# A tiled 8192 x 8192 transpose: TensorE's program half in two-turn loops, with a semaphore for each PSUM bank

## The chip, the cores and the metric

One core of a Trainium2 chip runs the kernel. The metric is the device time of one execution in microseconds (us), median of several runs. Ratios are the mean time of one kernel's fast runs over the mean of the other's fast runs of the same rounds, so they are not quite the ratio of the medians quoted here. Profiles are of one execution; their span is about 1.8 us shorter than the time.

## The reference

```python
def setup_inputs():
    return {"x": np.random.randn(8192, 8192).astype(np.float32)}

def reference(x):
    return np.transpose(x)
```

268.4 MB are read and 268.4 MB are written. There is no arithmetic.

## The kernel before

The input is cut into 128 chunks of 128 rows x 4096 columns (2 MiB). A chunk is loaded to one of three input buffers. TensorE transposes its 32 squares of 128 x 128, four to a PSUM bank, eight banks in all. ScalarE copies the even banks and VectorE the odd ones to store regions in SBUF; a region gathers the same output rows over eight chunks, so that a store writes long rows. One region is full after each chunk and is stored (2 MiB). Nine regions serve eight open windows. SyncE issues all loads and stores, on one queue.

```python
for t, (s, c) in enumerate(chunks):
    nc.tensor.wait_ge(s_ld[t % NIN], 16 * (t // NIN + 1))
    closing = []
    for q in [(c + k) % NR for k in range(NR)]:       # the closing bank first
        if q not in window:
            ...                                        # take a free region r
            if stored[r]:
                (nc.scalar, nc.vector)[q % 2].wait_ge(s_st[r], 16 * stored[r])
        ...
        if bank[n % NPS] is not None:
            nc.tensor.wait_ge(*bank[n % NPS])          # count of the copying engine
        for b in range(B):
            last = nc.tensor.transpose(...)
        last.then_inc(s_pe, 1)
        n += 1
        (nc.scalar, nc.vector)[e].wait_ge(s_pe, n)
        ...                                            # copy the bank to its region
        cp.then_inc(s_cp[e], 1)
        ...
    for q, e, count in closing:
        nc.sync.wait_ge(s_cp[e], count)
        ...                                            # store the region
    if t + NIN < len(chunks):
        nc.sync.wait_ge(s_pe, n)
        load(t + NIN)
```

Of the kernel before, what the change touches and what calls it, by code (L numbers as in the profile page):

```python
# [24 lines left out]
def wide_dma(nc, eng, queue, out, in_):  # L25


    return eng.add_instruction(
        mybir.InstDMACopy(
            mode="Copy",  # L30
            name=nc.get_next_instruction_name(),
            engine=eng.engine,
            ins=[physical(in_)],
            outs=[physical(out)],
            queue=queue,
        )
    )


@with_exitstack  # L40
def kernel(
    ctx: ExitStack,
    tc: tile.TileContext,
    x: bass.AP,
    out: bass.AP,
):






    nc = tc.nc
    P = 128
    N, M = x.shape
    assert x.shape == out.shape[::-1]
    dt = x.dtype

    S = 32
    B = 4  # L60
    W = 8
    NR = S // B
    NIN = 3
    NREG = 9
    NPS = 8
    CH = N // P
    J = S * P

    with tc.tile_critical():  # L69
        nc.alloc_sbuf_tensor("pad", [P, 32], dt)  # L70
        ident = nc.alloc_sbuf_tensor("ident", [P, P], dt).ap()
        ins = [nc.alloc_sbuf_tensor(f"in{k}", [P, J], dt).ap() for k in range(NIN)]
        regs = [nc.alloc_sbuf_tensor(f"reg{k}", [P, B * W * P], dt).ap() for k in range(NREG)]
        pss = [nc.alloc_psum_tensor(f"ps{k}", [P, B * P], dt).ap() for k in range(NPS)]

        s_id = nc.alloc_semaphore("s_id")
        s_ld = [nc.alloc_semaphore(f"s_ld{k}") for k in range(NIN)]
        s_st = [nc.alloc_semaphore(f"s_st{k}") for k in range(NREG)]
        s_pe = nc.alloc_semaphore("s_pe")
        s_cp = [nc.alloc_semaphore("s_cpa"), nc.alloc_semaphore("s_cpv")]  # L80

        nc.gpsimd.memset(ident, 0.0).then_inc(s_id, 1)  # L82
        nc.gpsimd.wait_ge(s_id, 1)
        nc.gpsimd.affine_select(  # L84
            out=ident,
            in_=ident,
            compare_op=mybir.AluOpType.not_equal,
            fill=1.0,
            base=0,
            pattern=[[-1, P]],  # L90
            channel_multiplier=1,
        ).then_inc(s_id, 1)
        nc.tensor.wait_ge(s_id, 2)

        chunks = [(s, c) for s in range(M // J) for c in range(CH)]

        def load(t):
            s, c = chunks[t]
            nc.sync.dma_start(
                out=ins[t % NIN], in_=x[c * P:(c + 1) * P, s * J:(s + 1) * J]  # L100
            ).then_inc(s_ld[t % NIN], 16)

        for t in range(NIN):
            load(t)

        n = 0
        copied = [0, 0]
        bank = [None] * NPS
        free = list(range(NREG))
        stored = [0] * NREG  # L110
        window = {}
        stores = 0
        for t, (s, c) in enumerate(chunks):
            nc.tensor.wait_ge(s_ld[t % NIN], 16 * (t // NIN + 1))
            closing = []
            for q in [(c + k) % NR for k in range(NR)]:
                if q not in window:


                    span = (q - c) % W + 1  # L120
                    r = free.pop(0)
                    parts = [(s, c, min(c + span, CH))]
                    if c + span > CH and t + span < len(chunks):
                        parts.append((s + 1, 0, c + span - CH))
                    window[q] = (t, r, parts)
                    if stored[r]:
                        (nc.scalar, nc.vector)[q % 2].wait_ge(s_st[r], 16 * stored[r])
                t0, r, parts = window[q]
                k = [p[0] for p in parts].index(s)
                base = B * P * sum(z - a for _, a, z in parts[:k])  # L130
                _, a, z = parts[k]
                rows = (z - a) * P
                view = regs[r][:, base:base + B * rows].rearrange("p (b i) -> p b i", b=B)
                ps = pss[n % NPS]
                e = q % 2
                if bank[n % NPS] is not None:
                    nc.tensor.wait_ge(*bank[n % NPS])
                for b in range(B):
                    last = nc.tensor.transpose(  # L139
                        ps[:, b * P:(b + 1) * P],  # L140
                        ins[t % NIN][:, q * B * P + b:(q + 1) * B * P - B + b + 1:B],
                        ident,
                    )
                last.then_inc(s_pe, 1)
                n += 1
                o = view[:, :, (c - a) * P:(c - a + 1) * P]
                i = ps.rearrange("p (b i) -> p b i", b=B)
                (nc.scalar, nc.vector)[e].wait_ge(s_pe, n)  # L148
                if e == 0:
                    cp = nc.scalar.copy(out=o, in_=i)  # L150
                else:
                    cp = nc.vector.tensor_copy(out=o, in_=i)  # L152
                cp.then_inc(s_cp[e], 1)
                copied[e] += 1
                bank[(n - 1) % NPS] = (s_cp[e], copied[e])
                if t + 1 == t0 + sum(z - a for _, a, z in parts):
                    closing.append((q, e, copied[e]))
            for q, e, count in closing:
                t0, r, parts = window.pop(q)
                nc.sync.wait_ge(s_cp[e], count)  # L160
                base = 0
                for s_, a, z in parts:
                    rows = (z - a) * P
                    j0 = s_ * J + q * B * P
                    dst = out[j0:j0 + B * P, a * P:a * P + rows]
                    dst = dst.rearrange("(q b) i -> q b i", q=P)
                    src = regs[r][:, base:base + B * rows]
                    base += B * rows
                    if stores:
                        st = wide_dma(nc, nc.sync, "qSPDynamicHW", dst, src)  # L170
                    else:
                        st = nc.sync.dma_start(
                            out=dst, in_=src.rearrange("q (b i) -> q b i", b=B)
                        )
                    st.then_inc(s_st[r], 16)
                    stores += 1
                    stored[r] += 1
                free.append(r)
            if t + NIN < len(chunks):
                nc.sync.wait_ge(s_pe, n)  # L180
                load(t + NIN)
        for r in range(NREG):
            nc.sync.wait_ge(s_st[r], 16 * stored[r])
# [30 lines left out]
```

## Time and profile before

| | before |
|---|---|
| time, median of 3 runs | 1265.92 us (1265.42 to 1266.32) |
| data queue's packets, share of 16 DMA engines | 99.9% |
| mean rate over the span | 425 GB/s |
| TensorE, VectorE, ScalarE busy | 59%, 28%, 24% |
| packets that carried TensorE's program | 32, of 16 KB |

The lines themselves stand in the prediction below. A row of nines on DMA says that each engine had a packet in flight nearly always; only the GB/s row beneath says how fast the packets moved, and an experiment below shows the two part (e8: nines at 404 GB/s).

### The profile page before, as it was taken

The numbers are of one execution on the slowest core, as the hardware profiler recorded it, in microseconds if no ns is written. First come the engines' busy times: TensorE is split into PE (matmuls) and PEld (weight loads), VectorE is DVE, ScalarE is ACT, GpSimd is POOL, SyncE is SP. The second block draws the span as 40 slices with busy tenths as digits, with TensorE's granted clock in tenths as the row PEclk, the third lists the DMA queues.
The fourth block names the chain that finished last, engine by engine and source line by source line (L and its number), as shares of the span: only waits on it lengthen the run. The fifth ranks groups of instructions, "written<-read, shape, count | busy, mean of one in ns | idle before, by whom it ended". The sixth has DMA issues, their size and how long they took to land.

```text
span 1263.6 us, 9807 instructions
## 1 busy us (share of the span) xinstructions
PE 748.9 (59%) x4096; PEld 724.9 (57%) x4096; DVE 353.9 (28%) x512; ACT 301.2 (24%) x513; POOL 0.7 (0%) x6
## 2 busy tenths in 40 slices
PE   6666555665566656565566655665556656565561
PEld 5566555665566656565566655665555655565551
DVE  3322222232222322222222322222222322223220
ACT  3222222222222222222222222222222222222220
POOL 0000000000000000000000000000000000000000
PEclk9876868677677776868677767777777686868776
DMA  9999999999999999999999999999999999999998
GB/s 385 427 427 430 428 427 430 429 430 429 428 428 428 430 429 429 428 430 429 427 427 412 430 429 428 429 429 429 429 429 429 429 429 427 431 429 429 430 427 351
DMA packets 39308, 537.51 MB, mean 425 GB/s; under 512 B 4320, under 2 KB 4832, under 8 KB 6240
## 3 DMA queue, kind: packets, MB, share of 16 engines
q1 hardware_dynamic: 39264, 536.89, 99.9%
q8 instruction: 32, 0.52, 0.2%
q14 instruction: 12, 0.10, 0.0%
HBM read 268.44 MB, written 268.44 MB: 425 GB/s over the span
## 4 chain that ended last, share of the span: by engine, by line
DMA 78%; PE 19%; issue 0%; ACT 0%; SPq 0%; ACTq 0%
DMA in<-in_x_dram 78%; PE ps L139 19%; ACT reg L150 0%; SPq L209 0%; SPq L69 0%; ACTq L148 0%
## 5 line engine op out<-in xcount | busy, mean ns | idle before, releaser
L139 PE MATMUL ps<-ident,in 128*128 128x128 f32 x4096 | 748.9, 365 | 486.8 <-DMA in<-in_x_dram 486.8
L139 PEld LDWEIGHTS ps<-ident,in 128*128 128x128 f32 x4096 | 724.9, 219 | 510.7 <-DMA in<-in_x_dram 502.4
L152 DVE COPY reg<-ps 128x512 f32<-128x512 f32 x512 | 353.9, 691 | 882.1 <-PE ps L139 882.1
L150 ACT COPY reg<-ps 128x512 f32<-128x512 f32 x512 | 299.9, 586 | 934.3 <-PE ps L139 932.6
L150 ACT ACT_TABLE_LOAD x1 | 1.3, 1283 | 0.9 <-SPq L69 0.9
L84 POOL TENSOR_SCALAR_AFFINE_SELECT ident<-ident 128x128 f32<-128x128 f32 x1 | 0.3, 292 | 0.2 <-POOL ident L82 0.2
L82 POOL MEMSET ident<- 128x128 f32 x1 | 0.2, 204 | 0.5 <-SPq L69 0.5
L198 POOL MEMSET const-bfloat16-1.0<- 128x1 bf16 x1 | 0.1, 101 | 0.0
L198 POOL MEMSET const-uint8-127<- 128x1 uint8 x1 | 0.1, 101 | 0.0
L198 POOL MEMSET const-float32-0.0<- 128x1 f32 x1 | 0.1, 98 | 0.2 <-issue 0.2
L198 POOL MEMSET const-float32-1.0<- 128x1 f32 x1 | 0.1, 98 | 0.0
## 6 DMA issues: line engine op xcount, KB each, us to landing
in<-in_x_dram SPq DMA_DIRECT2D x128, 2048.0 KB, 23.6
out_dram<-reg SPq DMA_DIRECT2D x114, 2048.0 KB, 22.6
out_dram<-reg SPq DMA_DIRECT2D x4, 1792.0 KB, 19.9
out_dram<-reg SPq DMA_DIRECT2D x4, 1536.0 KB, 19.6
out_dram<-reg SPq DMA_DIRECT2D x4, 1280.0 KB, 19.6
out_dram<-reg SPq DMA_DIRECT2D x4, 1024.0 KB, 19.4
out_dram<-reg SPq DMA_DIRECT2D x4, 768.0 KB, 17.9
out_dram<-reg SPq DMA_DIRECT2D x4, 512.0 KB, 16.2
```

What stands on the lines that cost most here:

```text
L82: nc.gpsimd.memset(ident, 0.0).then_inc(s_id, 1)
L84: nc.gpsimd.affine_select(out=ident, in_=ident, compare_op=mybir.AluOpType.not_equal, fill=1.0, base=0, pattern=[[-1, P]], channel_multipl ...
L139: last = nc.tensor.transpose(ps[:, b * P:(b + 1) * P], ins[t % NIN][:, q * B * P + b:(q + 1) * B * P - B + b + 1:B], ident,)
L150: cp = nc.scalar.copy(out=o, in_=i)
L152: cp = nc.vector.tensor_copy(out=o, in_=i)
L198: nc = _bacc.Bacc("TRN2", target_bir_lowering=False, num_devices=1)
```

## The change

The intent: in the kernel before, the counts that TensorE waits for grow from chunk to chunk, so no two chunks have the same instructions, and they can't be turns of a loop. With a semaphore for each bank, and TensorE taking back what it waited for, each turn of a loop looks the same, and half of the program can be put in loops of two turns. The sequence of stores and loads on SyncE keeps each store ahead of the next load, as it was. For the loop body to repeat every six chunks, the banks go 0 to 7 in every chunk.

```diff
+        def transposes(t):
+            k = t % NIN
+            nc.tensor.sem_inc(s_ld[k], -16).wait_op(s_ld[k], 16, "sem-ge")
+            for q in range(NR):
+                if t:
+                    nc.tensor.sem_inc(s_bank[q], -1).wait_op(s_bank[q], 1, "sem-ge")
+                for b in range(B):
+                    tr = nc.tensor.transpose(...)
+                    if b == B - 1:
+                        tr.then_inc(s_pe, 1)
 ...
+        first = T % (2 * TURNS * BODY)                 # 8; BODY 6, TURNS 2
+        for t in range(first):
+            transposes(t)
+        for t0 in range(first, T, 2 * TURNS * BODY):
+            with nc.Fori(0, TURNS, engines=[nc.tensor.engine]):
+                for t in range(BODY):
+                    transposes(t0 + t)
+            for t in range(TURNS * BODY, 2 * TURNS * BODY):
+                transposes(t0 + t)
 ...
-            for q in [(c + k) % NR for k in range(NR)]:
+            for q in range(NR):
 ...
-                cp.then_inc(s_cp[e], 1)
+                if closes(window[q], t):
+                    cp.then_inc(s_cp[e], 1)
+                    ...
+                    eng.wait_ge(s_cp[e], copied[e])
+                    eng.sem_inc(s_bank[q], 1)
+                else:
+                    cp.then_inc(s_bank[q], 1)
```

More of the change, by code (lines that the diff above doesn't have):

```diff
@@ L63 @@
     NIN = 3
+    BODY = 2 * NIN
+    TURNS = 2
     NREG = 9
-    NPS = 8
     CH = N // P
@@ L73 @@
         regs = [nc.alloc_sbuf_tensor(f"reg{k}", [P, B * W * P], dt).ap() for k in range(NREG)]
-        pss = [nc.alloc_psum_tensor(f"ps{k}", [P, B * P], dt).ap() for k in range(NPS)]
+        pss = [nc.alloc_psum_tensor(f"ps{k}", [P, B * P], dt).ap() for k in range(NR)]
         s_id = nc.alloc_semaphore("s_id")
@@ L78 @@
         s_st = [nc.alloc_semaphore(f"s_st{k}") for k in range(NREG)]
+        s_bank = [nc.alloc_semaphore(f"s_bank{q}") for q in range(NR)]
         s_pe = nc.alloc_semaphore("s_pe")
@@ L92 @@
         ).then_inc(s_id, 1)
-        nc.tensor.wait_ge(s_id, 2)
         chunks = [(s, c) for s in range(M // J) for c in range(CH)]
@@ L101, in load @@
             ).then_inc(s_ld[t % NIN], 16)
+        def transposes(t):
[5 more added lines that the diff above has]
+                for b in range(B):
+                    tr = nc.tensor.transpose(
+                        pss[q][:, b * P:(b + 1) * P],
+                        ins[k][:, q * B * P + b:(q + 1) * B * P - B + b + 1:B],
+                        ident,
+                    )
+                    if b == B - 1:
+                        tr.then_inc(s_pe, 1)
+        T = len(chunks)
+        nc.tensor.wait_ge(s_id, 2)
+        first = T % (2 * TURNS * BODY)
[7 more added lines that the diff above has]
+                transposes(t0 + t)
         for t in range(NIN):
             load(t)
-        n = 0
         copied = [0, 0]
-        bank = [None] * NPS
         free = list(range(NREG))
@@ L112, with closes @@
         stores = 0
+        def closes(w, t):
+            t0, r, parts = w
+            return t + 1 == t0 + sum(z - a for _, a, z in parts)
         for t, (s, c) in enumerate(chunks):
-            nc.tensor.wait_ge(s_ld[t % NIN], 16 * (t // NIN + 1))
             closing = []
-            for q in [(c + k) % NR for k in range(NR)]:
+            for q in range(NR):
+                e = q % 2
+                eng = (nc.scalar, nc.vector)[e]
                 if q not in window:
@@ L122 @@
                     parts = [(s, c, min(c + span, CH))]
-                    if c + span > CH and t + span < len(chunks):
+                    if c + span > CH and t + span < T:
                         parts.append((s + 1, 0, c + span - CH))
@@ L126 @@
                     if stored[r]:
-                        (nc.scalar, nc.vector)[q % 2].wait_ge(s_st[r], 16 * stored[r])
+                        eng.wait_ge(s_st[r], 16 * stored[r])
                 t0, r, parts = window[q]
@@ L131 @@
                 _, a, z = parts[k]
-                rows = (z - a) * P
-                view = regs[r][:, base:base + B * rows].rearrange("p (b i) -> p b i", b=B)
-                ps = pss[n % NPS]
-                e = q % 2
-                if bank[n % NPS] is not None:
-                    nc.tensor.wait_ge(*bank[n % NPS])
-                for b in range(B):
-                    last = nc.tensor.transpose(
-                        ps[:, b * P:(b + 1) * P],
-                        ins[t % NIN][:, q * B * P + b:(q + 1) * B * P - B + b + 1:B],
-                        ident,
-                    )
-                last.then_inc(s_pe, 1)
-                n += 1
+                view = regs[r][:, base:base + B * (z - a) * P].rearrange("p (b i) -> p b i", b=B)
                 o = view[:, :, (c - a) * P:(c - a + 1) * P]
-                i = ps.rearrange("p (b i) -> p b i", b=B)
-                (nc.scalar, nc.vector)[e].wait_ge(s_pe, n)
+                i = pss[q].rearrange("p (b i) -> p b i", b=B)
+                eng.wait_ge(s_pe, t * NR + q + 1)
                 if e == 0:
@@ L152 @@
                     cp = nc.vector.tensor_copy(out=o, in_=i)
-                cp.then_inc(s_cp[e], 1)
-                copied[e] += 1
-                bank[(n - 1) % NPS] = (s_cp[e], copied[e])
-                if t + 1 == t0 + sum(z - a for _, a, z in parts):
+                if closes(window[q], t):
+                    cp.then_inc(s_cp[e], 1)
+                    copied[e] += 1
                     closing.append((q, e, copied[e]))
+                    eng.wait_ge(s_cp[e], copied[e])
+                    eng.sem_inc(s_bank[q], 1)
+                else:
+                    cp.then_inc(s_bank[q], 1)
             for q, e, count in closing:
@@ L178 @@
                 free.append(r)
-            if t + NIN < len(chunks):
-                nc.sync.wait_ge(s_pe, n)
+            if t + NIN < T:
+                nc.sync.wait_ge(s_pe, (t + 1) * NR)
                 load(t + NIN)
```

## The prediction

> **What bounds the kernel now.** I read the page from the top: busy shares, the 40 slices, the DMA queues, the chain, and only then the waits and one turn of the timeline. The busy shares and the slices:
>
> ```profile
> PE 748.9 (59%) x4096; PEld 724.9 (57%) x4096; DVE 353.9 (28%) x512; ACT 301.2 (24%) x513; POOL 0.7 (0%) x6
> ...
> DMA  9999999999999999999999999999999999999998
> GB/s 385 427 427 430 428 427 430 429 430 429 428 428 428 430 429 429 428 430 429 427 427 412 430 429 428 429 429 429 429 429 429 429 429 427 431 429 429 430 427 351
> ...
> q1 hardware_dynamic: 39264, 536.89, 99.9%
> q8 instruction: 32, 0.52, 0.2%
> ...
> DMA 78%; PE 19%; issue 0%; ACT 0%; SPq 0%; ACTq 0%
> ```
>
> No compute engine passes 59%, while the DMA row is full in every slice and the rate is flat at 427 to 431 GB/s except at both ends and one dip (412). The data queue's packets fill 99.9% of sixteen engines' time. 536.9 MB at 429 GB/s is 1251 us of 1263.6; the rest is the first load, the dip and the end. The chain names loads and TensorE because it follows semaphores; what the waits and the timeline add is how far from the limit the engines are. TensorE and SyncE's waits, and one chunk:
>
> ```profile
> PE ps L139 <- DMA in<-in_x_dram: 486.8, 127, 8.3
> ACT reg L150 <- DMA out_dram<-reg: 1.7, 2, 1.1
> ...
> in<-in_x_dram SPq DMA_DIRECT2D x128, 2048.0 KB, 23.6
> out_dram<-reg SPq DMA_DIRECT2D x114, 2048.0 KB, 22.6
> ...
> 601.31 5.60 PE L139 MATMUL ps<-ident,in 128*128 128x128 f32 x32 [4.16 <-DMA in<-in_x_dram]
> ...
> 602.81 0.55 SPq L28 DMA_DIRECT2D out_dram<-reg  x1
> ...
> 606.94 0.34 SPq L99 DMA_DIRECT2D in<-in_x_dram  x1
> ```
>
> A chunk is one 2.097 MB load, 32 transposes in 8 banks, 8 copies and one 2.097 MB store. Each transfer needs 2.097/0.429 = 4.89 us, so the period is 9.78 us (601.31 and the next chunk at 611.07 agree: 9.76). TensorE works 5.60 us of it and waits 4.16 us for data: 127 waits, 486.8 us. A load lands 23.6 us after its issue, though it moves in 4.89: it stands behind 18.7 us of queued work. So a load or store may be issued many microseconds later without a DMA engine going idle.
>
> One finer reading. The trace holds sixteen completion events for each transfer. In the first load they lie 0.40 us apart, at 258 us 3.1 us, and from 962 us on 7.4 us; the last transfer's lie from 1256.0 to 1262.3 us. The lag grows in steps of about 1.4 us, one after each packet of the instruction queue, and settles on eight of the sixteen. So those eight set the end, and they carry all 32 instruction packets, four each. By the page a packet takes 0.2% x 16 x 1263.6 / 32 = 1.26 us (the share is rounded).
>
> [...] 0.52 MB in 32 packets is 16 KB each, and 4096 matmuls with 4096 weight loads are 32 x 256 instructions. [...]
>
> **The change part by part.**
>
> (1) TensorE's program. Built, it has 3136 written matmuls (98 chunks: 8, then five times 6 in a loop of two turns and 12 written out), still 4096 executed. Each wait becomes a semaphore decrement of its own, 9 a chunk, 877 written in place of 131. Instructions written: 2 x 3136 + 877 + some 30 = 7180 against 2 x 4096 + 131 + 10 = 8330, or 28 pages against 32.5. If each page is fetched once, some 28 packets: the eight slow engines still carry 3 or 4 each, at most one of 1.4 us saved. If the five jumps back refetch (a body is 440 instructions, 1.7 pages), the packets run to 128 x 73 / 256 = 36.5 [...]. [...]
>
> (2) TensorE's own time. Nine decrements a chunk at the 17 to 21 ns that VectorE's and ScalarE's semaphore instructions show are 0.2 us; if each also breaks the overlap of a weight load (226 ns median), 2 us. 5.6 becomes 5.8 to 7.8, under 9.76. [...] All lies in the 4.16 us of waiting or in the queue's 18.7 us: 0.
>
> (3) Bank order. Banks now go 0 to 7 in every chunk; before, the bank that closes came first. The store is issued after bank c mod 8: p x 0.70 us (5.60/8) later for p = 0 to 7, mean 2.45. The SyncE sequence of 270 transfers is the same in both builds, so each keeps its place in the ring: a store's time from issue to landing falls from 22.6 to about 20.2, and its landing does not move. Loads still go out at the end of TensorE's chunk, up to 1.3 us later when p = 7. 0 on the path.
>
> (4) A new wait. A window's first copy needs the region stored two chunks earlier. Before, that store went out 1.5 us into its chunk (602.81 - 601.31) and its copy was the last one two chunks later, 2 x 9.76 + 7 x 0.70 + 0.8 = 25.2 us; the store landed at 1.5 + 22.6 = 24.1. That just fits, hence two waits of 1.7 us in all. After, the copy is at place p + 1 (place 0 after p = 7), needed at 20.3 + 0.70(p + 1); the landing is still at 24.1. The wait is 3.1 - 0.7p for p = 0 to 4, none for 5 and 6, and 3.8 for 7: mean 1.5 us, some 180 us over 120 chunks. It holds back one copying engine. TensorE needs that bank only in the next chunk, and the chunk's closing bank belongs to the other engine, so neither the load nor the store is held up. Hidden.
>
> (5) A closing copy now waits for itself before it frees its bank: about 128 waits on engines 24 to 28% busy. 0.
>
> Sum: the transfers' 1263.6 us unchanged, -1.4 to +8.5 us from instruction packets, most weight on one or two more per slow engine: about +1.5, so **1267 us**.
>
> **The rivals.** A: the new region wait passes to TensorE and the loads. For it: it is long in sum (180 us) and the copies run in order. Against it: 3.8 us of delay plus four copies at 1.4 us is 9.4, just inside 9.76; even if a load goes 5 us late, 18.7 us stand before it on the slowest engine, some 11 on the fastest. It would need the queue to run dry: 1 to 4% if it did in many chunks. B: loops stall TensorE for fetches behind a full data queue. For it: an instruction packet takes about 1.3 us among the data and several may come one after another. Against it: five jumps only, and a stall must pass the 4 us slack and most of 15 us of queue to cost anything; 5 x 10 us of dry queue would be 4%, but I see nothing to make a stall of 25 us. C: the gain. Loops save instruction traffic, but all of it is 32/8 x 1.4 = 5.6 us on the slow engines, 0.4% of the time, so no version of this passes 2% faster.
>
> **Range and chances.** Unchanged packets with a little luck at the end: 1263 to 1265. [...] Run to run the kernel moves 0.9 us. So 1262 to 1275 for 8 in 10. Faster by 2% would be under 1240.6, which at 537 MB needs over 433 GB/s sustained from start to end: 0.01. Slower by 2% is over 1291: only rivals A or B, 0.02.
>
> **What would show it.** Right: rates of 427 to 431 in the slices and the data queue near 99.9%; stores' time to landing near 20 us; ScalarE and VectorE waiting for stores over 100 us in sum; TensorE still waiting some 3 to 4 us a chunk for loads; the count of instruction packets [...] telling which case of (1) holds. Wrong: slices below 420 GB/s, TensorE waiting on copies rather than loads, or loads to landing well under 20 us. The whole would be wrong if the queue is less deep than the median says, at the jumps above all.

The sum came to 1263.6 us and -1.4 to +8.5 us from instruction packets, of which it took +1.5, and was put at 1267 us. A page is what one packet of the instruction queue carries: 16 KB (0.52 MB in 32), or some 256 instructions, an estimate from 8330 written for 32 packets; the packets rose with the length of TensorE's program in the runs below (28 in the changed kernel, 36 in e3, 48 in e7, 64 in e4). That eight engines carry the packets, four each, is inference from the steps of the lag; the trace does not name engines.

## The result, and the profile after

The changed kernel took 1266.03 us (median of 6 runs, 1265.91 to 1266.5), the kernel before 1265.74 us (6 runs). The ratio of the fast runs is 1.0003, with a 95% interval of 0.999 to 1.0015: the same.

The page of the changed kernel, its rates, queues and median times to landing:

```profile
GB/s 384 428 428 428 429 430 428 430 430 429 429 429 429 429 429 428 430 430 430 427 426 415 429 429 428 431 430 429 428 430 428 430 430 428 429 429 431 429 423 338
...
q1 hardware_dynamic: 39264, 536.89, 99.9%
q8 instruction: 28, 0.46, 0.1%
...
in<-in_x_dram SPq DMA_DIRECT2D x128, 2048.0 KB, 22.8
out_dram<-reg SPq DMA_DIRECT2D x114, 2048.0 KB, 19.7
```

The rate is as flat as before. TensorE's program came in 28 packets in place of 32. A store's time from issue to landing fell from 22.6 to 19.7 us. That is no faster store: it is issued later, 4.3 us in the mean after its chunk's first transpose in place of 1.8 (traces, 200 to 1200 us), and waits less in the queue; a 16 KB packet took 611 ns in the median in both traces.

The waits of the changed kernel (engine, line, releaser: us in total, times, longest), then the two lines of the kernel before that the prediction does not show:

```profile
ACT reg L173 <- PE ps L114: 758.2, 390, 9.0
DVE reg L175 <- PE ps L114: 757.9, 402, 10.4
...
PE ps L114 <- PEq L112: 484.1, 126, 5.8
ACT reg L173 <- DMA out_dram<-reg: 184.2, 44, 8.9
DVE reg L175 <- DMA out_dram<-reg: 130.2, 38, 8.1
```

```profile
ACT reg L150 <- PE ps L139: 932.6, 510, 7.3
DVE reg L152 <- PE ps L139: 882.1, 511, 10.3
```

A wait of 314 us (184.2 + 130.2) for stores is new, and it took the place of waits for TensorE: ScalarE's fell by 174.4 us, VectorE's by 124.2. In groups by line, the idle time before the copies hardly moved: 934.3 to 942.5 us on ScalarE, 882.1 to 888.9 on VectorE. They wait for something else, about as long.

Two of the profile's views change their look for a reason that is not time. TensorE's wait for loads, 486.8 us before, now stands under "PEq L112" (484.1 us). L112 is the decrement for a bank, which follows the one for the load (L109). That the time is still spent on loads has to be checked, since waiting on copies would have been a sign against the prediction: in the trace every L109 runs 0.03 us after its load landed, and the first L112 of a chunk 0.15 us after that (0.32 at most). TensorE waits for loads. And the chain that ended last stops at once, as it does not follow those instructions:

```profile
PE 0%; DVE 0%; issue 0%
PE ps L114 0%; DVE reg L175 0%
```

Such a chain says nothing of what bounds the kernel; the rates and waits have to.

Chunk by chunk on TensorE in the changed kernel, around the first jump back (start, us, then the idle time before it). By the load that each chunk waited for, the row at 112.25 is chunk 13, the last of a body, and 122.02 is chunk 14, the first of the second turn:

```profile
102.39 6.54 PE L114 MATMUL ps<-ident,in 128*128 128x128 f32 x32 [3.46 <-PEq L112]
112.25 5.22 PE L114 MATMUL ps<-ident,in 128*128 128x128 f32 x32 [3.33 <-PEq L112]
122.02 5.43 PE L114 MATMUL ps<-ident,in 128*128 128x128 f32 x32 [4.55 <-PEq L112]
131.78 5.57 PE L114 MATMUL ps<-ident,in 128*128 128x128 f32 x32 [4.33 <-PEq L112]
```

The chunks start 9.77 and 9.76 us apart across the jump: no stall shows. The loop's own instructions, of TensorE's sequencer, have a line too (ns, shortest/median/longest):

```profile
L128 PEldq COMPARE_BRANCH  x10: 76/148/238, 115.3 to 1115.9; - x10
```

One by one, the five jumps that were taken lasted 214 to 238 ns, the five that were not 76 to 83.

One reading has no view of its own. Each transfer ends with sixteen completion events in the trace, as many as the page counts DMA engines. I take them for one of each engine. The trace does not say which engine an event belongs to, only when it came, so that is an inference, and so is every engine that is said to lag below; I sort the events and read the lag of the latest behind the earliest. For the transfer that ended nearest to 1200 us, and for the last store:

```
                     packets   lag of the last / next to last / median   last store's completions
                     of TensorE's   behind the first, near 1200 us       first / next to last / last
                     program        (us)                                 (us from the span's start)
before               32        7.4 / 7.3 / 4.4                           1256.0 / 1262.2 / 1262.3
changed              28        8.2 / 8.0 / 4.1                           1258.4 / 1263.1 / 1263.3
```

In the kernel before, eight engines lag by 5.1 to 7.4 us near 1200 us. In the changed kernel six of the eight most lagging lie at 4.3 to 5.5, less than before, but two still at 8.0 and 8.2. The kernel's last instructions wait for all sixteen of every store (16 * stored[r]), so the latest decide.

### The profile page after: what moved, and what is told of

The parts are those of the page before. It is cut to its first block, busy times and chain, and to the rows that moved or that the text cites. A ratio compares the mean times of both kernels' runs of the same rounds, so it can differ in the third digit from the quotient of the medians.

```text
span 1264.6 us, 10983 instructions
## 1 busy us (share of the span) xinstructions
PE 744.2 (59%) x4096; PEld 723.7 (57%) x4096; DVE 348.6 (28%) x512; ACT 293.6 (23%) x513; POOL 0.7 (0%) x6
## 5 line engine op out<-in xcount | busy, mean ns | idle before, releaser
L114 PE MATMUL ps<-ident,in 128*128 128x128 f32 x4096 | 744.2, 364 | 492.6 <-PEq L112 484.1
L175 DVE COPY reg<-ps 128x512 f32<-128x512 f32 x512 | 348.6, 690 | 888.9 <-PE ps L114 757.9
L173 ACT COPY reg<-ps 128x512 f32<-128x512 f32 x512 | 292.3, 588 | 942.5 <-PE ps L114 758.2
## 6 DMA issues: line engine op xcount, KB each, us to landing
in<-in_x_dram SPq DMA_DIRECT2D x128, 2048.0 KB, 22.8
out_dram<-reg SPq DMA_DIRECT2D x114, 2048.0 KB, 19.7
```

Of the source, the lines that this page charges most:

```text
L114: tr = nc.tensor.transpose(pss[q][:, b * P:(b + 1) * P], ins[k][:, q * B * P + b:(q + 1) * B * P - B + b + 1:B], ident,)
L173: cp = nc.scalar.copy(out=o, in_=i)
L175: cp = nc.vector.tensor_copy(out=o, in_=i)
```

## The experiments

Twelve runs were made, of nine kernels (two were run again for more traces). All gave correct results, and no run was in the slow state; the three single runs (e10 to e12) can't be classed, but their granted clocks, 0.742 to 0.749, are those of the kernel before. The times of the kernel before in the same three jobs were 1265.59, 1265.61 and 1265.69 us (medians of 9 runs each). The theory: two resources decide. The data queue decides the level, and it is deep enough to hide the new wait; the lag of the slowest DMA engine decides the last few us, and packets of TensorE's program are one cause of the lag. The rivals: the new wait costs something that saved packets pay back; or packets do not matter; or the loops stall TensorE.

### One part alone: bank order

```diff
 (in the kernel before)
-            for q in [(c + k) % NR for k in range(NR)]:
+            for q in range(NR):
```

> The kernel before with one part of the change alone: the banks go 0 to 7 in every chunk. Theory: this part alone makes the new wait of the copying engines for stores (314 us in the changed kernel against 1.7 before; expected 250 to 350 here), brings stores' median time to landing from 22.6 to about 20 us, and leaves the time at 1265.7 within 1 us, with 32 instruction packets as before. Rival (the waits come from the semaphore per bank or the loops): they stay under 20 us in sum here. Rival (the wait costs time that the saved packets paid back in the change): 1267 to 1269 here.

Measured: 1265.81 us, ratio 1.0001 (0.9987 to 1.0014), 32 instruction packets, stores at 19.9 us to landing. Its waits for stores:

```profile
ACT reg L150 <- DMA out_dram<-reg: 206.6, 46, 10.5
DVE reg L152 <- DMA out_dram<-reg: 165.2, 39, 9.3
```

Together 372 us, a little over the expected range, from this part alone and with no packets saved. The bank order is the cause of the new wait, and the wait costs nothing here. The rival of a cost that is paid back falls.

### Other parts alone: written out, and all in one loop

```diff
 (in the changed kernel: e3)
+        for t in range(T):
+            transposes(t)
 (in the changed kernel: e1)
+        first = T % BODY
+        for t in range(first):
+            transposes(t)
+        with nc.Fori(0, (T - first) // BODY, engines=[nc.tensor.engine]):
+            for t in range(BODY):
+                transposes(first + t)
```

> The changed kernel without its loops: TensorE's 128 chunks all written out, with the nine decrements a chunk kept. Theory: 36 or 37 instruction packets in place of 28, so four or five on each slow engine, time 1266 to 1267.5. Rival (the count of packets does not matter): 1266.0 as the changed kernel. It also shows what the decrements cost TensorE by themselves: 6.05 us a chunk as in the change, against 5.60 before at the like granted clock.

Measured: 1267.54 us (1267.42 to 1268.17), 36 packets, ratio to before 1.0016 (1.0003 to 1.003). Eight packets more than the changed kernel, one more for each of eight engines if they take turns (an inference, see below), went with 1.5 us more. Against the kernel before, of the same job, it is 1.95 us for four packets more. Chunks on TensorE are no longer for the decrements: from 300 to 600 us TensorE was busy for 179.9 us, against 183.6 before and 177.7 in the changed kernel, at granted clocks of 0.75, 0.73 and 0.76.

> The changed kernel with TensorE's program nearly all in one loop: 2 chunks written out, then 21 turns of 6. Wrong on nothing, same output. Theory (the end is set by eight DMA engines that carry the instruction packets, some 1.4 us each): a body of 440 instructions stays in TensorE's instruction store as it did in the change (28 packets for 28 pages), so 3 to 5 packets in all, the spread of the sixteen completions near the end falls from 8 us to 3 to 4, and the time falls by 3 to 5 us to 1261 to 1263. Rival 1 (every jump back refetches): 40 or more packets, time 1266 or more. Rival 2 (the lag of the eight has another cause or does not set the end): few packets, but 1265.5 to 1266.5 as now. Rival 3 (loops stall TensorE): its wait for loads falls and some chunks start late.

Measured: 1266.22 us (five runs from 1263.72 to 1267.77), two packets, no stall, and no gain. So packets fell as the theory had it and the time did not. The spread of completions in its trace tells why:

```
                     packets   last / next to last / median lag   last store: first / next to last / last
all in one loop      2         9.3 / 6.1 / 1.0                    1259.8 / 1261.1 / 1264.7
```

The median engine now lags 1.0 us in place of 4.1: the packets' lag is gone from the many. But five engines still lag by 4.1 us or more near 1200 us, and one of them lags 9.3 us and ends 3.6 us behind the next. Its lag grew steadily, by some 0.1 us a chunk, from 4.7 us near 780 to 9.6 near 1220 us, with no instruction packet at hand. So the count of packets was one cause of lag, not the only one, and my expectation was wrong in taking it for the one that sets the end. Two more traces of the same kernel were to tell whether the lone engine's lag sets the time.

> The loop-only kernel once more, for a second trace. Its five times ranged from 1263.7 to 1267.8 us, and its trace had fourteen engines within 2 us and one that lagged 9.3 us by itself. Theory (the single lagging engine's amount differs from run to run and sets the time): the last completion of the last store stays at about the time minus 3 us, and the lag of the slowest engine at 1200 us is larger in the slower run, about 1 us for 1 us. Rival (the time is set elsewhere): the lag is as before and the time differs, or the other way.

> As the run before, a third trace of the loop-only kernel: theory and rival as there.

```
                     time      last / next to last / median lag   last store: first / next to last / last
first                1267.77   9.3 / 6.1 / 1.0                    1259.8 / 1261.1 / 1264.7
second               1265.59   7.5 / 6.7 / 0.4                    1257.6 / 1262.0 / 1262.5
third                1264.74   7.1 / 6.1 / 0.9                    1256.8 / 1260.9 / 1261.6
```

(The expectation's "fourteen engines within 2 us" does not hold of the first trace's lags near 1200 us: eleven are, and five lag by 4 us or more, as five do in the two new ones.) The time is the last engine's last completion plus 3.1 us in all three (1267.77 - 1264.7, 1265.59 - 1262.5, 1264.74 - 1261.6). So much is built in, as the kernel waits for the sixteen completions of every store. The run with the larger lag is the slower: 2.2 us of lag went with 3.0 us of time between the first and the third. Three runs are few, but the other traces say the same. In all twelve with three input buffers and TensorE not the bound (e4 and e8 left out), the profiled run's time less the last engine's lag near 1200 us lies between 1257.6 and 1259.9 us, while the times go from 1264.74 to 1275.09 and the lags from 7.1 to 15.8. The median lag tells nothing of the kind: it is 0.4 to 1.0 in these three and 3.6 to 7.2 in the rest. That the latest of the sixteen completions sets the end is shown. Why one falls behind (by 9.3 us in the first of these traces) with nothing but data to move is not: the traces do not name engines, and I have no experiment that touches it.

### More packets: a dose

The kernel before, with idle semaphore instructions after the transposes of each bank, eight of them (e4) or four (e7):

```diff
                 last.then_inc(s_pe, 1)
+                for _ in range(4):                     # e7: range(2)
+                    nc.tensor.sem_inc(s_pad, 1)
+                    nc.tensor.sem_inc(s_pad, -1)
```

> The kernel before with 64 idle semaphore instructions added to each chunk on TensorE, which double its program: 64 instruction packets in place of 32, eight on each slow engine in place of four. Theory: +4 x 1.4 = +5.6 us, 1270 to 1272, spread of completions near the end 12 to 14 us. Rival (the packets' lag does not set the end): 1265.7. TensorE's chunk grows by 64 x about 20 ns = 1.3 us, well within its 4.16 us of waiting, so it should not become the bound; if the wait for loads nearly vanishes, the run tells less.

Measured: 1313.43 us, ratio 1.0377. This run missed its aim: TensorE became the bound. Its waits (first, ScalarE's for TensorE) no longer show TensorE waiting for loads:

```profile
ACT reg L154 <- PE ps L140: 992.9, 512, 7.4
...
PE ps L140 <- issue: 125.1, 435, 0.7
PE ps L140 <- DMA in<-in_x_dram: 8.4, 1, 8.4
```

It waited for a load once. I had counted 20 ns for an idle semaphore instruction, from the lines of VectorE and ScalarE. TensorE's own have a line:

```profile
L147 PEldq EVENT_SEMAPHORE  x4096: 51/51/51, 8.4 to 1294.3; - x196
```

Each takes 51 ns, and in the trace one starts 151 ns after another (median). Eight make 1.21 us, and a bank took 1.24 us, start to start, in the median, a chunk 10.05. So what bounds this kernel is the rate at which TensorE's sequencer gets through them. The granted clock was low as well, 0.56 against 0.75 before; with 1.21 of the 1.24 us accounted for, it is not needed as a cause. The run says nothing on packets, but it does say what happens when the 4.16 us of waiting are used up.

> The kernel before with 32 idle semaphore instructions a chunk on TensorE, half of the run that made TensorE the bound at some 10.2 us a chunk (there 64 cost 4.4 us, 69 ns each). A chunk should take about 7.9 us, under the period of 9.76, and the program 48 packets, six on each of eight DMA engines. Theory (instruction packets lag those eight and the most lagging engine sets the end): +2 x 1.4 = +2.8 us, 1267.5 to 1269. Rival (what sets the end is not the count of packets, as the loop-only kernel with 2 packets and 1266.2 us suggests): 1265 to 1266.5.

Measured: 48 packets; six runs, five of 1267.7 to 1268.3 us and the profiled one of 1275.09; median 1268.21. The chunk hardly grew (6.40 us at 602.44, and TensorE's waits for loads sum to 490.8 us), so half of the padding cost TensorE next to nothing, not the 2.2 us that I had scaled. Scaling was the error: four of these instructions take 4 x 0.151 = 0.60 us of the sequencer, less than the 0.70 us that a bank's transposes take anyway, and eight take more. The time without the odd run rose by 2.6 us (1268.2 - 1265.6), for two packets more on each of eight engines, as inferred: an estimate of 1.3 us a packet, as the theory had it (recorded ratio to before 1.002, 1.0006 to 1.0033). The odd run asked for a second trace.

> The half-padded kernel once more. Five of its six times were 1267.7 to 1268.3 us, and the profiled one 1275.1 with one engine 15.8 us behind, 6 us behind the next. Theory: a run without that lone engine is at 1268, and its slowest engine at 1200 us lags about 9.5 us and not alone. Rival (profiling itself adds the 7 us): 1275 again with the same lone engine.

```
                     time      last / next to last / median lag   last store: first / next to last / last
first                1275.09   15.8 / 9.4 / 7.2                   1265.6 / 1265.8 / 1272.0
second               1267.90   9.2 / 9.0 / 5.6                    1258.5 / 1264.6 / 1264.8
```

1267.90 us under the profiler, without a lone engine: it is not profiling that costs the 7 us. In the first run one engine ended 6.2 us behind the next; in the second, two ended together. The lone engine appears in a kernel with 48 packets as in one with 2, so it does not come from the loops.

### How far from the limit: regions, order, input buffers

```diff
 (in the changed kernel, one at a time)
-    NREG = 9
+    NREG = 8                                           # e5
-            (load after the stores of the chunk)
+            (load ahead of the stores of the chunk)    # e6
-    NIN = 3
+    NIN = 2                                            # e8, with 16 chunks written out first
```

> The changed kernel with 8 store regions in place of 9, so that a window's first copy needs the store of the very last chunk, not of the one before it. Theory (what a copying engine waits for is off the path, because the load waits for TensorE alone and TensorE needs the held bank only a chunk later): the waits of ScalarE and VectorE for stores grow from 314 us to over 700 in sum, TensorE begins to wait for copies, stores' time to landing falls below 19 us, and yet three transfers, some 14 us, still lie in the queue when a store lands, so the time stays within 0.3% of 1265.6 and the slices at 428 to 430 GB/s. Rival A of the prediction (the region wait runs the queue dry): slices under 420 GB/s and 1275 us or more.

Measured: 1266.95 us, ratio 1.0009 (0.9996 to 1.0023). A load's time to landing fell from 22.8 to 19.4 us, a store's from 19.7 to 15.7. The waits for stores:

```profile
ACT reg L173 <- DMA out_dram<-reg: 792.6, 64, 17.6
DVE reg L175 <- DMA out_dram<-reg: 753.2, 62, 17.0
```

1546 us of waiting in place of 314, at no cost that the interval can tell from none. TensorE did begin to wait for copies, as expected: at the first bank of 17 chunks, 85 us in sum, and 126 times for over 1.2 us between two banks.

> The changed kernel with each chunk's load issued ahead of its store, undoing the order that the change's name speaks of. Theory: a store lands one transfer, 4.9 us, later against its chunk, so the region wait grows from 1.5 to 4 to 6 us a chunk (600 to 900 us in sum for both engines), hidden as before; time within 0.3% of 1265.6. Rival (the order of store and load is what keeps the wait hidden): 1270 us or more, with slices under 425 GB/s.

Measured: 1266.73 us, ratio 1.0008 (0.9994 to 1.0022), waits for stores of 783.1 and 754.9 us, over the range I gave, and stores at 24.5 us to landing. Issuing the store ahead of the load, or after it, makes no difference to the time that the interval can tell from none.

> The changed kernel with two input buffers in place of three (bodies of 4 chunks, 16 chunks written out first). It sizes the margin behind rival A. A load then goes out one load and one store later against its own use: loads' time to landing falls from 22.8 to about 13.5 us. When a chunk is done, 6 us after its load landed, 8.6 us of work are left on the slowest DMA engine and less than 1 us on the fastest, which is some 8 us ahead near the end. Theory: queue nearly dry on the fast engines alone, which do not set the end: 1265 to 1270 us. If the margin is smaller than I think: over 1275 with slices under 425 GB/s.

Measured: 1333.74 us, ratio 1.0543 (1.0528 to 1.0557). My figure was wrong by far. The rates and the data queue of this kernel:

```profile
DMA  8999999999999999999999999999999999999998
GB/s 337 375 406 427 402 426 403 407 413 386 428 402 381 427 388 428 407 397 421 382 425 408 411 419 398 427 398 404 413 393 430 385 404 408 386 426 414 404 414 360
...
q1 hardware_dynamic: 39264, 536.89, 98.8%
```

Read the two rows together: the share stays at nines, and the rate drops to 404 GB/s. In the trace, 8.7% of the 16 KB packets took over 640 ns, against 0.6% in the kernel before, where the median is 611 ns in both; 211 of them took exactly 1199 ns. What they took beyond 616 ns is 54 us for each engine, against 4 before, and the time rose by 68. It would be easy to say that these packets start on drained engines, but the trace doesn't bear it out. Of the 101 issues between 100 and 620 us, 100 found one earlier transfer (44) or two (56) that not even the fastest engine had finished; in the kernel before it was three or four, with eight store regions two or three (once four). The queue is shallow here, not empty. The padded kernel e4, at one or two as well, shows the same: 7.1% of its packets over 640 ns, and some 417 GB/s. Why packets take longer behind a shallow queue stays open. TensorE had its full wait (562.7 us in sum), so it was not the bound. My error was one of counting. With two input buffers the store of chunk t - 2 goes out ahead of the load of t, so when that load lands, only the store of t - 1 and the load of t + 1 are left, 9.8 us by the estimate of 4.89 us a transfer, and not 14.6. With 5.5 us until the next load is issued (600.68 to 606.20 in its timeline), 4.3 us are left, less than one transfer. Three input buffers hold the margin; the ninth region is not needed for it (e5: ratio 1.0009).

### A candidate to beat both

The loop-only kernel with the closing bank first; the body must then be 24 chunks long.

```diff
-    BODY = 2 * NIN
+    BODY = 8 * NIN
-            for q in range(NR):
+            for q in [(t + k) % NR for k in range(NR)]:
```

> The candidate to beat both: the loop-only kernel with the closing bank first again, as before. Bank order then repeats every 8 chunks and input buffers every 3, so the body is 24 chunks, some 1754 instructions or 6.9 pages of 256, run five times after 8 written out. Theory: no region wait (under 10 us in sum, stores back at some 22.6 us to landing) and, if the body stays in TensorE's store, some 9 instruction packets; time 1262 to 1266, the low end where no single DMA engine lags by itself. Rival (a body of 6.9 pages does not stay): 37 packets or more and 1266 to 1268.

Measured: 1266.3 us, ratio 1.0001 (0.9988 to 1.0015). The region wait went, as expected. But 27 packets came, between the 9 of a body that stays and the 37 of one fetched anew each turn (estimates, at 256 instructions a packet), and some jumps took long (the lines of waits, packets and the loop's branch, then TensorE's chunks around the first jump):

```profile
ACT reg L171 <- DMA out_dram<-reg: 1.1, 1, 1.1
...
q8 instruction: 27, 0.44, 0.1%
...
L127 PEldq COMPARE_BRANCH  x5: 76/235/5940, 291.1 to 1234.8; - x5
...
287.97 5.56 PE L114 MATMUL ps<-ident,in 128*128 128x128 f32 x32 [4.41 <-PEq L112]
299.28 6.57 PE L114 MATMUL ps<-ident,in 128*128 128x128 f32 x32 [5.76 <-PEq L112]
```

The packets' times show which turns were fetched: nine came in the second turn (292 to 500 us), none in the third, nine in the fourth (764 to 973 us), none in the fifth but one at its end. The jumps into the second and fourth turn took 5.94 and 5.89 us, those into the third and fifth 0.24 and 0.23. So the stall of rival B is real in the turns that were fetched. After the first, the next chunk started 11.31 us after the one before it and not 9.76; the queue hid that. Why every second turn stayed is not shown. No version here beats the kernel before. The best single run was one of the loop-only kernel, at 1263.72 us, 0.15% under the median before, and its others reach above 1267.

## Why the prediction was right

The level was right: the transfers keep 428 to 430 GB/s, and 1266.03 us lies 0.97 under the figure of 1267, inside the range. The sum as written does not reach 1267: it starts from 1263.6 us, which is the span, and 1.8 us more are needed for the time. With them the figure is the time before plus 1.5 us, and those 1.5 did not come for the reason given, as part (1) tells: that the figure came so close is partly luck.

Part (1), TensorE's program: of its three cases the first one came, 28 packets, as many as the estimate of the written pages. I had put most weight on the second, refetches at the jumps, and that was a guess that no trace had shown; the trace of the changed kernel speaks against it: no packet over 28 and no stall at the jump (chunks 9.77 and 9.76 us apart). The +1.5 us in the sum stands for refetches that did not happen; a body of 1754 instructions did show such jumps, 5.9 us each (e9). The worth of a packet, an estimate, held: 1.3 us for one more on each slow engine by the half-padded kernel, 1.5 by the written-out one, against the 1.4 read from the steps in the trace. The packet itself is shorter than the 1.26 us that the rounded share gave: 0.94 to 1.04 us in the trace before, but for the first one (1.49). That four saved packets gained nothing agrees with "at most one of 1.4 us saved", and simple counting would explain it. The packets' durations repeat every eight packets (1.03, 1.03, 1.01, 0.95, 0.94, 1.00, 1.00, 0.99, then again), as if eight engines took turns; no trace names them. If they do, 32 packets are four on each, 28 still four on half of them, 36 five on half of them, 48 six on each: by this estimate the busiest engine carries 4, 4, 5 and 6, and the times lay 0.3, 2.0 and 2.6 us above that of the kernel before.

Part (2), TensorE's own time: within its slack, as said, though the unit cost of a semaphore instruction was too small. On TensorE one takes 51 ns and starts 151 ns after the last (e4, median), so nine a chunk are up to 1.4 us of its sequencer and not 0.2; 890 of the 1016 decrements for banks start while a transpose runs, and they cost nothing visible: a chunk's transposes took 5.82 us in the mean, against 5.85 before. The ten branches took 1.5 us in all: five of 214 to 238 ns, five of 76 to 83.

Part (3), bank order: a store's time to landing was forecast at about 20.2 us and came to 19.7, in the changed kernel and nearly so (19.9) with this part alone.

Part (4), the new wait: there, from bank order alone, and hidden, as said. The 180 us stand against 314 in the profile, but these are two quantities. The term counted only the delay that the store adds to a window's first copy. The profile counts the whole idle stretch before that copy under its last releaser, so stretches that were waits for TensorE before changed their label, as the nearly unchanged idle sums suggest. The delay itself can be read from the trace, from the end of a bank's transposes to the start of its copy: 154 us over the first copies, by place 3.7 us (forecast 3.8), then 2.9, 1.9, 1.1, 0.6, 0.3, 0.1 and 0.1 (forecast 3.1, 2.4, 1.7, 1.0, 0.3, 0 and 0). The term was close.

Rival A could be made as large as 1546 us of waiting without a cost that the interval can tell from none. What does go with a cost is a shallow queue, one or two earlier transfers at an issue (1333.74 us), and it took the loss of an input buffer to get there (e8, where no copy waits for a store). Rival B, stalls at loops, did not appear with a body of 440 instructions, even with 21 turns (e1: two packets in all, jumps of at most 0.24 us). With 1754 it did, 5.9 us at two of four jumps, and was hidden (1266.3 us). Rival C was right that the gain is small, but its reason holds only for the trace of before: with two packets (e1), engines that lag for another reason, by 7.1 to 9.3 us, set the end, and the 5.6 us do not come.

## What to carry to other kernels

Where the transfers fill the span at a flat rate, ask of each change how late it makes the next issue, and compare that with the work left in the queue when it is issued; count that work transfer by transfer in the order of issue. A wait that is new in the profile may have only taken the name of an old one: compare the engine's idle sum (934.3 and 942.5 us on ScalarE here) before you call it a cost. Read the rate together with the busy share, since the share alone stayed full where the rate had fallen (404 GB/s in e8). And take the cost of an instruction from the line of the engine that runs it: TensorE's semaphore instructions took 51 ns, not the 17 to 21 of its neighbours.
